# Group two's down projection in seven products, with weight sums made in group one's FFN

## The chip, the cores and the metric

The kernel runs on one core of one Trainium2 chip. Its engines work side by side from queues of their own: TensorE (PE: matmuls, PEld: the loading of their weights), VectorE (DVE), ScalarE (ACT), GpSimd (POOL) and SyncE (SP), which issues most DMA transfers. The metric is the device time of one execution in microseconds (us), lower is better; the number of a kernel is the median of its runs.

## The reference

One layer of an encoder with two attention mixers, run for 1024 prompt rows and 32 sample rows with the same weights. The FFN at its end is what matters here (D_MODEL 1024, D_FF 4096, all float32):

```python
h = x + jnp.einsum('bld,de->ble', m, w_out)
u = jnp.einsum('bld,df->blf', rmsnorm(h, g_ffn), w_up)
return h + jnp.einsum('blf,fd->bld', jnp.square(jax.nn.relu(u)), w_down)
```

## The kernel before

**Numbers.** TensorE works on pairs: each float32 operand is split into a high part h (a copy in the type float32r, made on ScalarE) and a low part l = x - h (made on POOL or VectorE). A product of 128 x 128 weights with a slice of activations is three matmuls (`three`): wh·xh, wh·xl, wl·xh. A weight *block* is 128 partitions x 512: four such 128 x 128 tiles. Blocks are loaded by SyncE to a raw tile (`wst`, bufs=3), then split to `wh`, `wl` (a ring of WB = 5 pairs).

**Groups.** The 1056 rows are run in two groups: group one has 512 rows (one slice of 512 columns), group two 544 (two slices c = 0, 1 of 272). Group one's FFN runs (`ffn_group`) while part of group two's attention (`late`) is fed in beside it, a piece each few blocks (`beside`). Then come group two's branch and output projections and its FFN.

**Group one's FFN.** Eight rounds q. Ups: a row of u is 8 x 3 matmuls of 512 columns into one of two PSUM banks (`pj`), relu and the rest on ScalarE, POOL (`ru`) and VectorE (`xl`). Downs: `go_down(e, q)` adds 512 rows of D_FF (four tiles, 12 matmuls) and VectorE adds the bank to the output tile y.

**Group two's FFN.** Its ups (`go_up_quad`) are done in the Strassen-Winograd form: a 2 x 2 quad of weight blocks times the two halves of the activations and the two slices is seven products of 12 matmuls instead of eight. That needs four sums of weight blocks (`quad_units`): they are made by loading a block by SyncE and adding others to it with accumulating transfers from POOL's queue (tile `raw`, bufs=10). The activations' sums (`g.sums`) are made once. Downs are plain: 8 x 8 x 2 of 12 matmuls into banks `pd`. One up quad and four downs alternate.

**Order.** Nothing is issued by hand. `Plan` records every instruction with a rank (FAST for what frees a bank, PREP for weights, MAIN, FILL for matmuls) and an estimated cost, and then issues for each engine the ready one of the best rank; it counts POOL and those VectorE instructions that have all inputs on chip (`locks`) as excluding each other. The order is fixed when the kernel is built; each engine keeps to it.

Of the kernel before, what the change touches and what calls it, by code (L numbers as in the profile page):

```python
# [19 lines left out]
D = 1024  # L20
# [21 lines left out]
WB = 5  # L42
SPLIT = 6
AHEAD = 0
KEEP = (6, 7)
# [373 lines left out]
class Layer:  # L419
# [9 lines left out]

    def split(self, h, l, x):  # L430

        self.nc.scalar.copy(h, x)
        self.nc.gpsimd.tensor_sub(l, x, h.bitcast(F32))
# [40 lines left out]
    def column_block(self, units, rhs, done, chunks, kn=KB, tag="pj"):  # L474

        nc = self.nc
        for c, cs in enumerate(chunks):
            n = cs.stop - cs.start
            ps = self.bank(tag)
            with nc.rank(FILL):  # L480
                for k in range(kn):
# [3 lines left out]
                    self.three(ps[:, :n], wh[:, ks], wl[:, ks], xh, xl, k == 0, k == kn - 1)  # L485
            with nc.rank(FAST):
                done(c, cs, ps[:, :n])
# [9 lines left out]
    def run(self):  # L497
# [34 lines left out]
        self.dh = dt([KB, 128, T], "dh")  # L532

# [104 lines left out]
        self.ffn_group(g2)  # L638
# [745 lines left out]
    def quad_units(self, f):  # L1384

        nc, a, w = self.nc, self.a, self.quads
        with nc.rank(PREP):
            src = lambda i, j: a["w_up"][f + i, j]
# [11 lines left out]
            def part(z, pool, tag, bufs, eng):  # L1400
                h = nc.tile(pool, [128, 512], F32R, tag + "h", bufs=bufs)
                l = nc.tile(pool, [128, 512], F32R, tag + "l", bufs=bufs)
                nc.scalar.copy(h, z)
                eng.tensor_sub(l, z, h.bitcast(F32))
                return h, l

            V, G = nc.vector, nc.gpsimd
            z = load((1, 0), (1, 1))
            z3 = load((0, 0), (1, 0))
            a11, a22, a12 = load((0, 0)), load((1, 1)), load((0, 1))  # L1410
            s1 = part(z, w, "s", 4, V)
            load((0, 0), out=z)
            s2 = part(z, w, "s", 4, V)
            load((0, 1), out=z)
            s3 = part(z3, w, "s", 4, V)
            s4 = part(z, w, "s", 4, G)
            p11 = part(a11, self.wpool, "w", WB, G)
            p12 = part(a12, self.wpool, "w", WB, G)
            p22 = part(a22, self.wpool, "w", WB, G)
        return p11, p12, p22, s1, s2, s3, s4  # L1420

# [10 lines left out]
    def square(self, g, ps, uh, ul, sign=1.0):  # L1432

        nc = self.nc
        r = g.tmp("ru", "pb", 3)
        nc.scalar.activation(r, ps, AF.Relu, scale=sign)
        if not g.i:
            nc.gpsimd.tensor_mul(r, r, r)
            nc.scalar.copy(uh, r)
            nc.vector.tensor_sub(ul, r, uh.bitcast(F32))  # L1440
            return
        nc.vector.scalar_tensor_tensor(ps, ps, sign, r, op0=ALU.mult, op1=ALU.mult)
        nc.scalar.copy(uh, ps)
        nc.vector.tensor_sub(ul, ps, uh.bitcast(F32))

    def ffn_group(self, g, late=iter(())):
        nc, a, i = self.nc, self.a, g.i
        n = g.n
        rb2 = g.acc

        def scales():

            for c in range(len(g.chunks)):
                ps = self.bank("pj")
                nc.tensor.matmul(ps[:, :n], self.ones, g.acc[c], start=True, stop=True)
                with nc.rank(FAST):
                    v = g.tmp("rv", "pb", 3)
                    nc.vector.tensor_scalar(v, ps[:, :n], 1.0 / D, EPS, op0=ALU.mult, op1=ALU.add)
                    nc.vector.reciprocal(rb2[c], v)

        nq, us = DFF // 512, {}

        def go_up(f):
            units = [self.unit(a["w_up"][f, j]) for j in range(2)]
            us[f] = uh, ul = g.mh[:, f % 8], g.ml[:, f % 8]
            self.column_block(units, lambda k, cs: (g.h[:, k, cs], g.l[:, k, cs]),
                              lambda c, cs, ps: self.square(g, ps, uh[:, cs], ul[:, cs]), g.chunks)

        def go_up_quad(f):

            a11, a12, a22, s1, s2, s3, s4 = self.quad_units(f)
            for i in range(2):
                us[f + i] = g.mh[:, (f + i) % 8], g.ml[:, (f + i) % 8]
            ta, tb, tc, td = ([(th[:, k], tl[:, k]) for k in range(4)] for th, tl in g.sums)
            x = lambda j, c: [(g.h[:, 4 * j + k, c * n:c * n + n], g.l[:, 4 * j + k, c * n:c * n + n]) for k in range(4)]

            def product(w, xs, ps=None):
                first = ps is None
                if first:
                    ps = self.bank("pj")[:, :n]  # L1480
                with nc.rank(FILL):
                    for k in range(4):
                        ks = slice(k * 128, k * 128 + 128)
                        self.three(ps, w[0][:, ks], w[1][:, ks], *xs[k], first and k == 0, k == 3, skip_group_check=True)
                return ps

            def keep(ps):
                t = nc.tile(self.op, [128, g.w], F32, "part", tag="o32", bufs=4)[:, :n]
                with nc.rank(FAST):
                    nc.scalar.copy(t, ps)  # L1490
                return t

            def done(i, c, out, ps, more=None):
                cs = slice(c * n, c * n + n)
                uh, ul = us[f + i]
                with nc.rank(FAST):
                    if more is not None:
                        nc.vector.tensor_add(out, ps, more)
                    self.square(g, out, uh[:, cs], ul[:, cs], -1.0 if i else 1.0)

            px = product(a11, x(0, 0))
            p1 = keep(px)
            pz = product(s1, ta)
            p5 = keep(pz)
            product(s2, tb, px)
            u2 = keep(px)
            product(s4, x(1, 1), pz)
            done(0, 1, pz, pz, u2)
            py = product(a12, x(1, 0))
            done(0, 0, py, py, p1)  # L1510
            product(s3, tc, px)
            done(1, 1, self.bank("pj")[:, :n], px, p5)
            product(a22, td, px)
            done(1, 0, px, px)

        def go_down(e, q):
            units = [self.unit(a["w_down"][e, q])]

            def done(c, cs, ps):
                y = g.y[:, e, cs]  # L1520
                if q == 0:
                    nc.scalar.copy(y, ps)
                    return
                if q < nq - 1:
                    nc.vector.tensor_add(y, ps, y)
                    return
                if e < KB // 2:
                    nc.vector.tensor_add(ps, ps, y)
                    y = hx_of(e, cs)
                nc.vector.tensor_mul(ps, ps, rb2[c])  # L1530
                nc.vector.tensor_add(g.y[:, e, cs], ps, y)
                nc.sync.dma_start(self.o["yT"][:, e, slice(g.lo + cs.start, g.lo + cs.stop)], g.y[:, e, cs])

            if q == nq - 1 and e >= KB // 2:
                for c, cs in enumerate(g.chunks):
                    y = g.y[:, e, cs]
                    nc.gpsimd.tensor_mul(y, y, rb2[c])
                    nc.gpsimd.tensor_add(y, y, hx_of(e, cs))
            self.column_block(units, lambda k, cs: (us[4 * q + k][0][:, cs], us[4 * q + k][1][:, cs]), done, g.chunks,
                              kn=4, tag="pd" if g.i else "pj")  # L1540

        def hx_of(e, cs):

            return g.h.bitcast(F32)[:, e, cs]

        def reload():

            with nc.rank(PREP):
                nc.sync.dma_start(g.h.bitcast(F32), self.dh[:, :, g.lo:g.lo + g.w].rearrange("e p t -> p e t"))
# [14 lines left out]
        if g.i:  # L1564
            go_up_quad(0)
            self.squares(g)
            go_up_quad(2)
            for q in range(nq):
                if q == 2:
# [106 lines left out]
```

## Time and profile before

| | us |
|---|---|
| median of three runs | 1766.61 (1764.76 to 1770.34) |
| the profiled execution | 1765.07 |
| its span, first to last instruction | 1763.3 |
| TensorE busy | 1739.2 (99%) |
| POOL / VectorE / ScalarE busy | 1051.8 / 1047.3 / 977.7 |

The granted TensorE clock is 1.00 throughout. Group one's FFN lies from about 860 to 1290 us, the late attention beside it until about 1115; group two's branch and output from 1290 to 1392, and its FFN from there to the end. Windows and groups of instructions are in us from the span's start; tiles have their names from the code, and nearly all instructions have the line of the one helper that issues them. Durations of matmuls overlap (they are pipelined), so their rate is read from counts.

### The profile page before, as it was taken

What the parts mean: (1) busy time and instruction counts of PE and PEld (TensorE: products, weight loads), DVE (VectorE), ACT (ScalarE), POOL (GpSimd) and SP (SyncE); (2) the same over time, 40 slices, a digit from 0 to 9 for tenths busy, and PEclk for the clock granted to TensorE, in tenths of its full rate; (3) what the DMA queues carried; (4) which work ended last, traced back from release to release, by engine and by line L of the source; (5) the groups of instructions that cost most, each with busy time, mean ns of one, the idle gap of its engine ahead of it and who ended that gap; (6) DMA issues with size and microseconds to landing.
All of it is one profiled execution on the core that took longest, in us unless ns stands there. A gap on an engine that the chain in (4) does not pass through costs nothing.

```text
span 1763.3 us, 32590 instructions
## 1 busy us (share of the span) xinstructions
PE 1739.2 (99%) x11394; PEld 1598.1 (91%) x11394; DVE 1047.3 (59%) x2284; ACT 977.7 (55%) x2145; POOL 1051.8 (60%) x902
## 2 busy tenths in 40 slices
PE   8999999999999999999999999999999999999999
PEld 7999999999899888888888888888899999999998
DVE  7555578999665645789646555222347853544445
ACT  7444598983255776677666455533336654444441
POOL 3623232435366675899965455675759876666655
PEclk9999999999999999999999999999999999999999
DMA  7244451545566668555444443433487576666624
GB/s 256 74 132 119 114 175 64 143 140 152 170 177 169 173 182 229 180 171 173 121 130 119 130 145 99 147 108 97 144 262 205 152 178 149 155 151 154 156 67 138
DMA packets 169908, 264.53 MB, mean 150 GB/s; under 512 B 28944, under 2 KB 58224, under 8 KB 169744
## 3 DMA queue, kind: packets, MB, share of 16 engines
q1 hardware_dynamic: 160096, 245.33, 47.4%
q0 software_dynamic: 9216, 16.78, 5.9%
q8 instruction: 90, 1.47, 0.3%
q14 instruction: 74, 0.61, 0.1%
q10 hardware_dynamic: 432, 0.34, 0.1%
HBM read 207.87 MB, written 54.40 MB: 149 GB/s over the span
## 4 chain that ended last, share of the span: by engine, by line
PE 87%; DMA 5%; DVE 2%; POOL 2%; issue 1%; ACT 1%; SPq 0%; POOLq 0%; ACTq 0%; DVEq 0%
PE pj L410 54%; PE s L410 13%; PE pd L410 11%; PE t L410 5%; PE o L410 4%; DMA raw<-w_up 1%; DMA sg<-dg 1%; POOL wl L410 1%; DMA k<-dk 1%; POOL pb L410 1%; SPq L410 0%; DMA o<-do 0%; DMA xt<-x 0%; DVE pen L410 0%; DMA q<-dq 0%
## 5 line engine op out<-in xcount | busy, mean ns | idle before, releaser
L410 POOL TENSOR_TENSOR wl<-wst,wh 128x512 fp32r<-128x512 f32 x350 | 493.4, 1419 | 359.7 <-ACT wh L410 334.8
L410 PE MATMUL pj<-xh,wh 128*128 128x512 f32 (+1 forms) x1600 | 557.5, 349 | 0.4 <-DVE vt L410 0.3
L410 PE MATMUL pj<-xh,wl 128*128 128x512 f32 (+1 forms) x1600 | 557.0, 349 | 0.0
L410 PE MATMUL pj<-xl,wh 128*128 128x512 f32 (+1 forms) x1600 | 556.7, 348 | 0.1
L410 ACT CAST wh<-wst 128x512 fp32r<-128x512 f32 x350 | 216.7, 621 | 324.3 <-PE pj L410 158.8
L410 PEld LDWEIGHTS pj<-xh,wh 128*128 128x128 f32 x1600 | 300.8, 188 | 33.6 <-ACT xh L410 0.7
L410 PEld LDWEIGHTS pj<-xh,wl 128*128 128x128 f32 x1600 | 300.8, 188 | 33.2
L410 PEld LDWEIGHTS pj<-xl,wh 128*128 128x128 f32 x1600 | 301.1, 188 | 32.0 <-DVE xl L410 0.3
L410 PE MATMUL pd<-xh,wh 128*128 128x272 f32 x512 | 148.3, 290 | 0.6 <-ACT y L410 0.3
L410 PE MATMUL pd<-xl,wh 128*128 128x272 f32 x512 | 147.5, 288 | 0.0
L410 PE MATMUL pd<-xh,wl 128*128 128x272 f32 x512 | 147.2, 288 | 0.0
L410 DVE TENSOR_TENSOR tt<-t,tt 128x512 fp32r<-128x512 f32 (+2 forms) x168 | 100.5, 622 | 62.1 <-ACT tt L410 60.6
L410 ACT ACTIVATE junk<-score,cand 128x384 bf16<-128x384 f32 (+1 forms) x124 | 116.0, 936 | 9.8 <-DVE cand L410 7.7
L410 DVE TENSOR_TENSOR_SCAN rem<-rem 128x896 f32<-128x896 f32 (+6 forms) x66 | 114.7, 1762 | 10.3 <-ACT rem L410 9.9
L410 POOL TENSOR_TENSOR p<-p,rem 128x895 f32<-128x895 f32 (+6 forms) x66 | 100.5, 1537 | 24.7 <-DVE rem L410 24.6
L410 ACT CAST tt<-t 128x512 fp32r<-128x512 f32 (+2 forms) x168 | 85.2, 540 | 45.7 <-PE t L410 38.7
L410 PE MATMUL s<-wl,xh 128*128 128x256 f32 (+1 forms) x360 | 101.8, 285 | 0.2 <-POOL wl L410 0.2
L410 PE MATMUL s<-wh,xh 128*128 128x256 f32 (+1 forms) x360 | 100.3, 286 | 0.9 <-DVE small L410 0.7
L410 PE MATMUL s<-wh,xl 128*128 128x256 f32 (+1 forms) x360 | 100.8, 283 | 0.0
L410 PEld LDWEIGHTS o<-tt,v 128*128 128x128 f32 x640 | 93.3, 188 | 8.3
L410 PE MATMUL s<-k,q 128*128 128x384 f32 (+5 forms) x384 | 96.1, 357 | 4.5 <-DMA q<-dq 1.6
L410 PE MATMUL o<-tt,v 128*128 128x256 f32 (+1 forms) x640 | 98.8, 276 | 0.0
(259 smaller groups left out, 3845.4 us busy)
## 6 DMA issues: line engine op xcount, KB each, us to landing
wst<-w_down SPq DMA_DIRECT2D x128, 256.0 KB, 2.7
raw<-w_up SPq DMA_DIRECT2D x80, 256.0 KB, 3.0
q<-dq SPq DMA_DIRECT2D x64, 256.0 KB, 5.4
wst<-w_up SPq DMA_DIRECT2D x64, 256.0 KB, 2.6
raw<-w_up POOLq DMA_DIRECT2D x64, 256.0 KB, 4.5
k<-dk SPq DMA_DIRECT2D x48, 256.0 KB, 4.2
v<-dv SPq DMA_DIRECT2D x48, 256.0 KB, 3.9
wst<-w_g SPq DMA_DIRECT2D x42, 256.0 KB, 3.4
```

Source lines behind the costliest of these rows:

```text
L410: fn(*args, **kw)
```

## The change

- **Group two's downs** are done in seven products too (`ffn_quads`, with `up` and `down`). They work on sums of u's parts: after each up quad the seven sets U11, T1, T2, U22, T3, U21, T4 are made from the products and split (`parts`), in place of four. A down block i is seven products over 512 rows each, so 1024 rows of D_FF and 2 x 2 output tiles at a time; its seven results are gathered in y. The rounds become four: four up quads, then four down blocks.
- **The weight sums** of both matrices are made in group one's FFN (`sums`): VectorE adds the four raw blocks in place, four additions of 128 x 512 for each quad, 128 in all, and SyncE stores the four results to DRAM, 128 stores of 256 KB. Group two loads them like weights, 224 plain loads by SyncE; the 64 accumulating transfers of POOL's queue are gone.
- **Group one's FFN** takes its blocks in quads (`row`), the raw blocks from a ring of eight tiles (three `wst`, three `sg`, two halves of `rb`), and its downs 1024 rows deep (24 matmuls for a bank); VectorE adds to y in three rounds in place of seven. KEEP, which held two downs back, is gone.
- Group two's raw blocks turn through nine tiles (the same eight and one `raw`), its split pairs through seven (five `wh`/`wl` and two `sh`/`sl`), and the banks `pj` and `pd` through one ring of eight.

```diff
-    def quad_units(self, f):
-            def load(*blocks, out=None):
-                st = out
-                if out is None:
-                    st = nc.tile(w, [128, 512], F32, "raw", bufs=10)
-                    nc.sync.dma_start(st, src(*blocks[0]))
-                    blocks = blocks[1:]
-                for b in blocks:
-                    nc.gpsimd.dma_start(st, src(*b), accum_op=ALU.add)
-                return st
...
+    def late_scale(self, g, e, c, cs, ps, sign=1.0, out=None):
+        (nc.vector.tensor_add if sign > 0 else nc.vector.tensor_sub)(out, y, ps)
+        nc.vector.tensor_mul(out, out, g.acc[c])
+        nc.vector.tensor_add(y, out, g.h.bitcast(F32)[:, e, cs])
+        nc.sync.dma_start(self.o["yT"][:, e, slice(g.lo + cs.start, g.lo + cs.stop)], y)
...
+    def ffn_quads(self, g):
...
+        def weights(name, t, engs):
+            w11, w12, _, w22 = (a[name][i, t] for i in range(4))
+            s1, s2, s3, s4 = self.sums[name, t]
+            for z, eng in zip((w11, s1, s2, s4, s3, w12, w22), engs):
+                with nc.rank(PREP):
+                    wt = pair(load(z), eng)
+                yield wt
...
+        def up(q, j):
+            wt = weights("w_up", 4 * q + j, (G, V, G, G, V, G, G))
...
+            px = product(next(wt), x[0])
+            keep(p1, px)
+            pz = product(next(wt), x[1])
+            keep(p5, pz)
+            product(next(wt), x[2], px)
+            keep(u2, px)
+            product(next(wt), x[3], pz)
+                add(pz, pz, u2)
+                square(u12, pz, 1.0)
+            product(next(wt), x[4], px)
+            pw = turn("bank", banks)
+                add(pw, px, p5)
+                square(pw, pw, -1.0)
+                parts(U22[j], pw, V)
+                sub(pz, pw, u12)
+                parts(T3[j], pz, V)
+            py = product(next(wt), x[5])
+                add(py, py, p1)
+                square(py, py, 1.0)
+                parts(U11[j], py, V)
+                sub(t1, py, u12)
+                parts(T1[j], t1, G)
+                V.scalar_tensor_tensor(t2, t1, -1.0, pw, op0=ALU.mult, op1=ALU.subtract)
+                parts(T2[j], t2, G)
+            product(next(wt), x[6], px)
+                square(px, px, -1.0)
+                parts(U21[j], px, V)
+                V.scalar_tensor_tensor(px, t2, -1.0, px, op0=ALU.mult, op1=ALU.subtract)
+                parts(T4[j], px, V)
...
+        def down(q, i):
+            wt = weights("w_down", 4 * q + i, (V, G, V, G, V, G, V))
...
+            px = product(next(wt), u[0])
+            gather(0, 0, px, 1.0, 0)
+            pz = product(next(wt), u[1])
+            gather(1, 1, pz, -1.0, 0)
...
+            product(next(wt), u[6], px)
+            gather(1, 0, px, -1.0, 2)
+
+        for q in range(4):
+            for j in range(4):
+                up(q, j)
+                if q + j == 0:
+                    self.squares(g)
...
+            for i in range(4):
+                down(q, i)
...
+        def sums(name, t, w11, w12, w21, w22):
+            add = nc.vector.tensor_add
+            add(w22, w21, w22)
+            add(w21, w11, w21)
+            add(w11, w11, w22)
+            add(w12, w12, w11)
+            for out, z in zip(self.sums[name, t], (w22, w11, w21, w12)):
+                nc.sync.dma_start(out, z)
...
+        for q in range(4):
+            for go, name, step in ((lambda j, i, w: go_up(4 * i + j, w), "w_up", 1),
+                                   (lambda j, i, w: go_down(2 * j + i, q, w), "w_down", 0)):
...
+                for j in range(4):
+                    raw = []
+                    for i in range(2):
+                        st, units = row(name, 4 * q + j, i)
+                        raw += st
+                        go(j, i, units)
+                        beside(2)
...
+                    sums(name, 4 * q + j, *raw)
```

The two weight matrices are laid out in quads on the host (the same numbers in another order).

How the order moves, at three places. **VectorE, group one's downs.** Before, it had there only the additions to y and, for the ups, the low part of u (`xl<-ru,xh`):

```order
L410 TENSOR_TENSOR y_6537<-pj,y_6537 128x512
L410 TENSOR_TENSOR xl_95<-ru,xh_94 128x512
L410 TENSOR_TENSOR y_6537<-pj,y_6537 128x512 x5
L410 TENSOR_TENSOR xl_95<-ru,xh_94 128x512 x2
L410 TENSOR_TENSOR y_6537<-pj,y_6537 128x512
```

Now, in a down stretch without attention (raw, wst and rb are the tiles of the raw blocks):

```order
L409 TENSOR_TENSOR y_6665<-pj,y_6665 128x512 x2
L409 TENSOR_TENSOR raw<-wst,raw 128x512
L409 TENSOR_TENSOR wst<-wst 128x512
L409 TENSOR_TENSOR wst<-wst,raw 128x512
L409 TENSOR_TENSOR wst<-wst 128x512
L409 TENSOR_TENSOR y_6665<-pj,y_6665 128x512 x2
L409 TENSOR_TENSOR rb<-rb 128x512
L409 TENSOR_TENSOR rb<-raw,rb 128x512
L409 TENSOR_TENSOR raw<-raw,rb 128x512
L409 TENSOR_TENSOR raw<-raw 128x512
```

Four sums stand between each two additions to y, all with both inputs on chip.

**SyncE, group one's FFN.** Before, weights were loaded one after another, beside the attention's q, k, v and its stores do:

```order
L410 DMA do<-o 64x512
L410 DMA wst<-w_up 128x512 x3
L410 DMA wst<-w_down 128x512 x2
L410 DMA do<-o 64x512
L410 DMA wst<-w_down 128x512 x2
L410 DMA k<-dk 128x512 x2
```

Now (dw_up and dw_down are the sums in DRAM):

```order
L409 DMA dw_up_0_138<-rb 128x512
L409 DMA dw_up_2_140<-rb 128x512
L409 DMA dw_up_1_139<-raw 128x512
L409 DMA dw_up_3_141<-raw 128x512
L409 DMA rb<-w_up 128x512 x2
L409 DMA raw<-w_up 128x512 x2
L409 DMA dw_up_0_142<-raw 128x512
L409 DMA dw_up_2_144<-wst 128x512
```

The loads to a ring's tiles stand behind the stores of the sums that lay in them.

**VectorE, group two's FFN.** Before, a quad's steps lay among the downs' additions (`y<-pd,y`):

```order
L410 TENSOR_TENSOR y_14410<-pd,y_14410 128x272 x6
L410 TENSOR_TENSOR sl<-raw,sh 128x512
L410 TENSOR_TENSOR pj<-pj,part 128x272 x2
L410 SCALAR_TENSOR_TENSOR pj<-pj,ru 128x272
L410 TENSOR_TENSOR pj<-pj,part 128x272
L410 SCALAR_TENSOR_TENSOR pj<-pj,ru 128x272
L410 TENSOR_TENSOR xl_95<-pj,xh_94 128x272
```

Now, in a stretch of ups (ut and ut2 hold u's parts that are kept, ul and xl the low parts of the sets):

```order
L409 TENSOR_TENSOR pj<-pj,part 128x272
L409 TENSOR_TENSOR ut<-pj,ut 128x272
L409 TENSOR_TENSOR wl<-wst,wh 128x512
L409 SCALAR_TENSOR_TENSOR pj<-pj,ru 128x272
L409 TENSOR_TENSOR pj<-pj,ut 128x272
L409 SCALAR_TENSOR_TENSOR ut_16511<-ut,pj 128x272
L409 TENSOR_TENSOR wl<-rb,wh 128x512
L409 TENSOR_TENSOR xl_223<-pj,xh_222 128x272
L409 TENSOR_TENSOR ul<-pj,uh 128x272
L409 SCALAR_TENSOR_TENSOR pj<-pj,ru 128x272
```

No downs lie between a quad's steps; the next quad's steps and weights do. TensorE has 192 matmuls less in the whole list.

More of the change, by code (lines that the diff above doesn't have):

```diff
@@ L428, in bank, with turn @@
         return self.nc.tile(self.pp[tag], [128, 512], F32, tag, tag="pj" if tag == "pd" else tag, bufs=n)
+    def turn(self, what, ways):
+        n = self.turns.get(what, 0)
+        self.turns[what] = n + 1
+        return ways[n % len(ways)]()
     def split(self, h, l, x):
@@ L480, in column_block @@
             with nc.rank(FILL):
-                for k in range(kn):
+                for i, k in enumerate(order or range(kn)):
                     wh, wl = units[k // 4]
@@ L532, in run @@
         self.dh = dt([KB, 128, T], "dh")
+        self.sums = {(w, t): [dt([128, 512], f"d{w}{t}_{i}") for i in range(4)] for w in ("w_up", "w_down") for t in range(16)}
+        self.turns = {}
         self.wpool = nc.open("w")
@@ L1430, in squares, with scales @@
                 self.nc.gpsimd.tensor_add(g.ss, g.ss, y)
-    def square(self, g, ps, uh, ul, sign=1.0):
+    def scales(self, g):
         nc = self.nc
[L1435 to L1488, printed above, removed]
@@ new lines, in scales, with reload @@
+        for c in range(len(g.chunks)):
+            ps = self.bank("pj")
+            nc.tensor.matmul(ps[:, :g.n], self.ones, g.acc[c], start=True, stop=True)
+            with nc.rank(FAST):
+                v = g.tmp("rv", "pb", 3)
+                nc.vector.tensor_scalar(v, ps[:, :g.n], 1.0 / D, EPS, op0=ALU.mult, op1=ALU.add)
+                nc.vector.reciprocal(g.acc[c], v)
+    def reload(self, g, n=1):
+        with self.nc.rank(PREP):
+            for es in (slice(0, 2), slice(2, KB)) if n > 1 else (slice(0, KB),):
+                self.nc.sync.dma_start(
+                    g.h.bitcast(F32)[:, es], self.dh[es, :, g.lo:g.lo + g.w].rearrange("e p t -> p e t"))
@@ new lines, in late_scale, with load, pair, product @@
+    def late_scale(self, g, e, c, cs, ps, sign=1.0, out=None):
+        nc = self.nc
+        y = g.y[:, e, cs]
+        out = ps if out is None else out
+        (nc.vector.tensor_add if sign > 0 else nc.vector.tensor_sub)(out, y, ps)
+        nc.vector.tensor_mul(out, out, g.acc[c])
+        nc.vector.tensor_add(y, out, g.h.bitcast(F32)[:, e, cs])
+        nc.sync.dma_start(self.o["yT"][:, e, slice(g.lo + cs.start, g.lo + cs.stop)], y)
+    def ffn_quads(self, g):
+        nc, a, w, n = self.nc, self.a, self.quads, g.n
+        V, G, add, sub = nc.vector, nc.gpsimd, nc.vector.tensor_add, nc.vector.tensor_sub
+        turn = self.turn
+        raws = [lambda: nc.tile(self.wpool, [128, 512], F32, "wst", bufs=3)] * 3
+        raws += [lambda: nc.tile(w, [128, 512], F32, "raw", bufs=1)]
+        raws += [lambda: self.rb[:, 0:512], lambda: self.rb[:, 512:1024]]
+        raws += [lambda: nc.tile(self.op, [128, g.w], F32, "raw", tag="sg", bufs=3)[:, :512]] * 3
+        pairs = [lambda: [nc.tile(self.wpool, [128, 512], F32R, z, bufs=WB) for z in ("wh", "wl")]] * WB
+        pairs += [lambda: [nc.tile(w, [128, 512], F32R, z, bufs=2) for z in ("sh", "sl")]] * 2
+        banks = [lambda: self.bank("pj")[:, :n]] * 6 + [lambda: self.bank("pd")[:, :n]] * 2
+        def load(src):
+            st = turn("raw", raws)
+            nc.sync.dma_start(st, src)
+            return st
+        def pair(st, eng):
+            h, l = turn("pair", pairs)
+            nc.scalar.copy(h, st)
+            eng.tensor_sub(l, st, h.bitcast(F32))
+            return h, l
+        def weights(name, t, engs):
[5 more added lines that the diff above has]
+                yield wt
+        def product(wt, xs, ps=None):
+            first = ps is None
+            if first:
+                ps = turn("bank", banks)
+            with nc.rank(FILL):
+                for k in range(4):
+                    ks = slice(k * 128, k * 128 + 128)
+                    self.three(ps, wt[0][:, ks], wt[1][:, ks], *xs[k], first and k == 0, k == 3, skip_group_check=True)
+            return ps
+        ta, tb, tc, td = ([(th[:, k], tl[:, k]) for k in range(4)] for th, tl in g.sums)
+        x = lambda j, c: [(g.h[:, 4 * j + k, c * n:c * n + n], g.l[:, 4 * j + k, c * n:c * n + n]) for k in range(4)]
+        x = [x(0, 0), ta, tb, x(1, 1), tc, x(1, 0), td]
+        old = [z.rearrange("p k t -> p (k t)").rearrange("p (i k t) -> p i k t", i=4, k=4) for z in (g.mh, g.ml)]
+        new = [nc.tile(w, [128, 3, 4, n], F32R, z) for z in ("uh", "ul")]
+        sets = [[z[:, i] for z in old] for i in range(4)] + [[z[:, i] for z in new] for i in range(3)]
+        u = [[(h[:, k], l[:, k]) for k in range(4)] for h, l in sets]
+        U11, T1, T2, U22, T3, U21, T4 = u
+        def parts(place, z, eng):
+            nc.scalar.copy(place[0], z)
+            eng.tensor_sub(place[1], z, place[0].bitcast(F32))
+        half = lambda name: nc.tile(self.op, [128, g.w], F32, name, tag="o32", bufs=4)
+        def up(q, j):
+            wt = weights("w_up", 4 * q + j, (G, V, G, G, V, G, G))
+            two, three_ = half("part"), half("ut")
+            u12, t1 = three_[:, :n], three_[:, n:]
+            t2 = half("ut2")
+            t2, u2 = t2[:, :n], t2[:, n:]
+            p1, p5 = two[:, :n], two[:, n:]
+            def keep(t, ps):
@@ L1502, in go_up_quad, with square @@
[L1502 to L1517, printed above, removed]
+            def square(out, ps, sign):
+                r = g.tmp("ru", "pb", 3)
+                nc.scalar.activation(r, ps, AF.Relu, scale=sign)
+                V.scalar_tensor_tensor(out, ps, sign, r, op0=ALU.mult, op1=ALU.mult)
```

175 lines of the change are left out of this document (88 added, 87 removed).

## The prediction

> **What bounds the kernel now.** I read the page's totals first, then its chain, then the windows, because a total says nothing of a stage.
>
> ```profile
> span 1763.3 us, 32590 instructions
> PE 1739.2 (99%) x11394; PEld 1598.1 (91%) x11394; DVE 1047.3 (59%) x2284; ACT 977.7 (55%) x2145; POOL 1051.8 (60%) x902
> PE 87%; DMA 5%; DVE 2%; POOL 2%; issue 1%; ACT 1%; SPq 0%; POOLq 0%; ACTq 0%; DVEq 0%
> ```
>
> TensorE is busy 99% of the span and 87% of the chain that ends last. A busy TensorE need not be one at its rate, so the windows (length; PE, PEld, DVE, ACT and POOL busy with counts; granted clock; DMA share; GB/s) must give the rate in the two stages that the change touches.
>
> ```profile
> 1200.00:1250.00 50.00, 50.00 (x222) 41.41 (x221) 13.14 (x15) 15.59 (x27) 29.12 (x24) 1.00 0.35 100
> 1300.00:1350.00 50.00, 48.30 (x379) 47.44 (x377) 25.60 (x46) 23.93 (x46) 37.93 (x38) 1.00 0.82 238
> 1400.00:1450.00 50.00, 48.11 (x373) 46.88 (x373) 29.98 (x48) 28.88 (x71) 39.34 (x34) 1.00 0.77 171
> 1440.00:1720.00 280.00, 280.00 (x2229) 279.69 (x2228) 119.65 (x263) 127.56 (x282) 166.92 (x145) 1.00 0.61 139
> ```
>
> Group one's FFN, once the late attention is out of it, runs one 512-column matmul each 50/222 = 225 ns; group two's runs one 272-column matmul each 280/2229 = 125.6 ns with no gap for 280 us. There a matmul less is worth 125.6 ns, whatever its recorded duration. The chain says the same: ups (pj) and downs (pd) alternate at 126 and 125 ns a matmul.
>
> ```profile
> 1553.38 8.92 PE pj L410 x71
> 1568.46 7.51 PE pd L410 x60
> ```
>
> The other engines have room in group two (DVE 43%, ACT 46%, POOL 60%). Only its beginning has gaps: 1.7 us idle in 1300 to 1350 and 1.9 us in 1400 to 1450.
>
> **The removal.** Group two's downs are
>
> ```profile
> L410 PE MATMUL pd<-xh,wh 128*128 128x272 f32 x512 | 148.3, 290 | 0.6 <-ACT y L410 0.3
> raw<-w_up POOLq DMA_DIRECT2D x64, 256.0 KB, 4.5
> 1309.02 11.20 DMA sg<-dg
> 1406.20 3.96 DMA raw<-w_up
> 1418.86 4.39 DMA raw<-w_up
> 1428.97 4.56 DMA raw<-w_up
> ```
>
> three such groups, 1536 matmuls. Seven products for 16 blocks of twelve matmuls are 16 x 7 x 12 = 1344. So 192 go: 192 x 125.6 ns = **24.1 us**. The ups keep their 1344, group one its 3 x 896.
>
> The 64 accumulating transfers on POOL's queue go too. At the start of the FFN they are links in the chain: load, add, split, and only then a matmul (the rows at 1406, 1419 and 1429). Their first ones also stand beside the gate loads of the branch stage, one of which takes 11.2 us to land. The sums are now ready in DRAM, so one plain load replaces such a chain. I bound this gain by 0 and by the 3.6 us of the two gaps, and take **2.0 us**, since half of them should have other causes.
>
> **The additions in group one.** 128 additions of 128x512 on VectorE, both inputs on chip, and 128 stores. The nearest rows, in the windows 1120 to 1290 (the last stretch without attention):
>
> ```profile
> L410 POOL TENSOR_TENSOR wl<-wst,wh 128x512 fp32r<-128x512 f32 x62 | 80.9, 1311 | 52.7 <-ACT wh L410 52.5
> L410 POOL TENSOR_TENSOR ru<-ru 128x512 f32<-128x512 f32 x15 | 15.6, 1043 | 0.0
> L410 DVE TENSOR_TENSOR xl<-ru,xh 128x512 fp32r<-128x512 f32 x15 | 20.5, 1367 | 63.7 <-ACT xh L410 63.7
> L410 DVE TENSOR_TENSOR y<-pj,y 128x512 f32<-128x512 f32 x28 | 19.4, 691 | 50.0 <-PE pj L410 49.8
> ```
>
> An addition from PSUM takes 691 ns. The one from two on-chip tiles (xl) takes 1367 there, though this timeline has it at 0.68 where POOL had been idle and at 1.37 where a POOL subtraction had begun 0.47 us before:
>
> ```profile
> 940.01 0.68 DVE L410 TENSOR_TENSOR xl<-ru,xh 128x512 fp32r<-128x512 f32 x1
> 941.38 1.13 POOL L410 TENSOR_SCALAR p<-p,nb 128x1024 f32<-128x1024 f32 x1 [1.82 <-PE pj L410]
> 1175.94 1.30 POOL L410 TENSOR_TENSOR wl<-wst,wh 128x512 fp32r<-128x512 f32 x1 [0.43 <-ACT wh L410]
> 1176.41 1.37 DVE L410 TENSOR_TENSOR xl<-ru,xh 128x512 fp32r<-128x512 f32 x1 [8.46 <-ACT xh L410]
> ```
>
> It ends 0.54 us after POOL's: it waited for POOL, so I count the two as taking turns. Per quad of four weight blocks TensorE needs 48 x 225 = 10.8 us. In an up quad the turns are 4 wl x 1.31 + 2 ru x 1.04 on POOL, and 2 xl x 0.68 + 4 sums x 0.69 on VectorE: 7.3 + 4.1 = 11.4 us, 0.6 over. In a down quad 5.2 + 2.8 = 8.0 us, 2.8 under. The split weights run five pairs ahead, 5 x 12 x 225 ns = 13.5 us of TensorE's work, more than four up quads fall behind (2.4 us). So it is covered by that lead; without it 16 x 0.6 = 10 us. Against the sums stand 32 evacuating additions that the 1024-deep downs save (0.69 each, 22 us of VectorE, from PSUM). The other place without cover is the start of that FFN, where POOL has no idle time:
>
> ```profile
> 840.00:850.00 10.00, 10.00 (x56) 8.66 (x56) 8.47 (x9) 6.62 (x14) 10.00 (x6) 1.00 0.53 168
> ```
>
> The first two quads' sums, 8 x 0.69 = 5.5 us, fall about there. Both together cost 0 to 15 us; I take **1.5**, because TensorE loses next to nothing at 840 to 850 though POOL is full. The stores, 128 x 256 KB over some 430 us, are 78 GB/s on top of the 100 at 1200 to 1250, less than the 238 GB/s of 1300 to 1350.
>
> The Trainium skill, SBUF — State Buffer, section "Who interferes with whom", states that a VectorE instruction with two SBUF inputs contends with a GpSimd one that reads SBUF, and that the later one blocks fully. That agrees with the 1.37 against 0.68 us above, and it speaks against this change: by it every sum is taken from POOL's time or POOL's from it.
>
> **The new order in group two.** Ups and downs no longer alternate: four up quads (84 matmuls, 10.5 us each), then four down blocks. What an up quad asks of each engine, from these rows:
>
> ```profile
> L410 DVE TENSOR_TENSOR sl<-raw,sh 128x512 fp32r<-128x512 f32 x36 | 25.6, 732 | 48.1 <-ACT sh L410 41.0 <-PE pj L410 7.0
> L410 DVE SCALAR_TENSOR_TENSOR pj<-pj,ru 128x272 f32<-128x272 f32 x49 | 21.5, 440 | 3.6 <-ACT ru L410 3.6
> L410 POOL TENSOR_TENSOR wl<-raw,wh 128x512 fp32r<-128x512 f32 x36 | 47.3, 1326 | 13.6 <-ACT wh L410 13.5
> L410 POOL TENSOR_TENSOR xl<-raw,xh 128x272 fp32r<-128x272 f32 x12 | 11.1, 946 | 0.0
> L410 ACT CAST wh<-raw 128x512 fp32r<-128x512 f32 x36 | 22.4, 622 | 25.0 <-issue 13.6 <-PE pj L410 5.5 <-POOL sl L410 2.5
> L410 ACT CAST xh<-pj 128x272 fp32r<-128x272 f32 x49 | 18.7, 384 | 0.5 <-DVE pj L410 0.4
> 1423.33 1.14 ACT L410 CAST sh<-raw 128x512 fp32r<-128x512 f32 x2 [1.68 <-DMA raw<-w_up]
> ```
>
> ScalarE: 7 casts of weights x 622 + 14 narrow ones (3 keeps, 4 relus, 7 casts) x 384 = 9.7 us of 10.5 by durations; two casts in 1.14 us show that they overlap by a tenth, so rather 8.8. VectorE: 2 x 0.73 + 16 x 0.44 = 8.5 us. POOL: 5 x 1.33 + 2 x 0.95 = 8.5 us, and with VectorE's two taking turns 10.0 us. Every one is under 10.5, none by much. In a down block the same sums are 4.4 (ScalarE), 4 x 0.73 + 7 x 0.44 = 6.0 (VectorE) and 3 x 1.33 = 4.0 us (POOL). A stretch of ups draws on seven split pairs, a quad's worth, so throughput is covered.
>
> What is less covered is the wait that opens inside a quad. The fifth product adds into a bank, VectorE reads it (add(pw, px, p5)), and the seventh adds into the same bank; between them stand the sixth product or the next quad's first, 12 x 125.6 ns = 1.5 us. That read stands on VectorE behind a weight subtraction, and these can be long where POOL is full:
>
> ```profile
> L410 DVE TENSOR_TENSOR sl<-raw,sh x48: 674/688/4162, 1308.9 to 1699.5; 128x512 fp32r<-128x512 f32 x48
> 1406.81 2.83 POOL L410 TENSOR_TENSOR wl<-raw,wh 128x512 fp32r<-128x512 f32 x2
> 1406.90 3.30 DVE L410 TENSOR_TENSOR sl<-raw,sh 128x512 fp32r<-128x512 f32 x1
> ```
>
> A median of 0.69 us costs nothing. One of 3.3 us delays the read past its 1.5 us by some 2 us. In the order a weight subtraction is among the three instructions ahead of that read in five of the 16 quads. I bound the loss by 0 and by 1 us in every quad, 16 us, and take **2.0 us**, 0.4 in each of the five: nearer to the median than to the long ones, since POOL no longer issues transfers there.
>
> **Sum**, against the profiled execution: span 1763.3 - 24.1 - 2.0 + 1.5 + 2.0 = 1740.7, and 1.8 us lie around it (1765.07 - 1763.3), 1742.5. The median of the runs, 1766.6, is 1.5 us above the profiled execution; I say **1743 us**. The end keeps its form: a last product, two VectorE steps and a store.
>
> **The rivals.** *The up stretches are bound by VectorE behind POOL.* For it: 10.0 of 10.5 us in turns, and 4.16 us as the longest subtraction. Against it: 280 us without a gap with the same seven products. Half the full price to all of it, 8 to 16 us: 1749 to 1757, say 1753.
>
> *VectorE and POOL taking turns bind group one.* By that port rule taken as a mechanism of this kernel, nothing is hidden: 10 us in the up quads and 5 at the start instead of 1.5, 1743 + 13.5 = 1756. For it: 11.4 against 10.8 us. Against: the down quads, and the lead. That is the rule of the skill's page named above; its time comes from the rows.
>
> *Slower: SyncE's queue in group one.* There each load of a raw block stands behind the stores of sums, which wait for VectorE, which waits for POOL; late, it holds up the next loads, the attention's among them. With eight raw buffers a quad's round must close within two quads, 21.7 us.
>
> ```profile
> wst<-w_down SPq DMA_DIRECT2D x128, 256.0 KB, 2.7
> dh<-y SPq DMA_DIRECT2D x8, 256.0 KB, 2.9
> ```
>
> Load 2.7, cast 0.6, four subtractions 5.2, sums 4 x 1.37 = 5.5 if each waits for POOL, store 2.9: 16.9 us. Above 21.7 every us costs one in two quads, 16 in all. The gain is eaten at 23.2; at 23.8 the kernel takes 1743 + 34 = 1777 us. For it: in 780 to 870 VectorE and POOL are nearly full. Against it: 4.8 us of slack, and quads that last longer while attention is mixed in.
>
> *More than I count:* both beginnings cleared and no new wait, 1765.1 - 24.1 - 3.6 = 1737.
>
> **Chances.** The forecast with its terms at their near ends (1738 to 1748) 0.58, the first rival 0.16, the second 0.09, slower 0.06, more 0.05; 0.06 is left for mixtures of the rivals that just cancel the gain. A measurement of this kernel tells 0.3%, 5.3 us, from no change: below 1761.3 is faster, so 0.88 faster, 0.06 the same, 0.06 slower. The range reaches from the favourable end to the second rival: 1735 to 1758.
>
> **What would show it.** 11202 matmuls, TensorE at 125.6 ns through all of group two, the time from the first up to the last down near 340 us, no accumulating transfers, sums at 0.7 to 1.4 us, and group one's FFN as long as before. Wrong would be: TensorE waiting for VectorE (pj) inside up stretches, for POOL's wl in group one, or SyncE's queue waiting for VectorE with wst landing late.

## The result, and the profile after

The changed kernel takes 1743.5 us (median of four runs, 1742.1 to 1745.5), the kernel before beside it 1765.7 (1763.4 to 1770.3): a ratio of 0.9872, with an interval of 0.9849 to 0.9895. Eight runs of the changed kernel, four of them taken later beside other experiments, have the same median. The profiled execution's span is 1741.1 us. The page's totals and the head of its chain:

```profile
span 1741.1 us, 32989 instructions
PE 1715.7 (99%) x11202; PEld 1574.6 (90%) x11202; DVE 1228.1 (71%) x2496; ACT 1018.6 (59%) x2241; POOL 1054.3 (61%) x862
PE 87%; DVE 5%; DMA 3%; issue 2%; POOL 2%; ACT 1%; SPq 0%; ACTq 0%; POOLq 0%; DVEq 0%
```

192 matmuls are gone, VectorE has 181 us more work, and TensorE is 99% busy as before. Three markers cut the span into stages: the first matmul of group two's branch (pj<-gh, by tile, before and then after), and the first copy of a product in group two's FFN (part<-pj):

```profile
L410 PE MATMUL pj<-gh,wh x34: 284/288/297, 1292.2 to 1304.6; 128*128 128x272 f32 x34
L410 ACT COPY part<-pj x6: 377/388/395, 1394.4 to 1407.7; 128x272 f32<-128x272 f32 x6
```

```profile
L409 PE MATMUL pj<-gh,wh x20: 284/288/297, 1297.5 to 1304.6; 128*128 128x272 f32 x20
L409 ACT COPY part<-pj x4: 381/390/394, 1395.8 to 1408.6; 128x272 f32<-128x272 f32 x4
```

| stage | before | after | difference |
|---|---|---|---|
| up to group two's branch | 1292.2 | 1297.5 | +5.3 |
| branch and output of group two | 102.2 | 98.3 | -3.9 |
| group two's FFN, to the span's end | 368.9 | 345.3 | -23.6 |
| span | 1763.3 | 1741.1 | -22.2 |

The same number of matmuls (7742) stands ahead of the first marker in both. So the forecast of 1743 was met by a sum of which two terms were badly sized, and these cancelled. The windows after, in the columns of the prediction's:

```profile
1150.00:1160.00 10.00, 8.82 (x39) 6.96 (x38) 6.96 (x6) 2.92 (x5) 10.00 (x7) 1.00 0.58 191
1160.00:1170.00 10.00, 8.86 (x39) 6.86 (x38) 7.35 (x5) 3.59 (x7) 10.00 (x8) 1.00 0.54 180
1200.00:1250.00 50.00, 50.00 (x222) 41.42 (x221) 32.88 (x29) 18.10 (x32) 39.26 (x29) 1.00 0.57 194
1300.00:1350.00 50.00, 50.00 (x400) 50.00 (x399) 24.83 (x46) 23.39 (x45) 36.19 (x34) 1.00 0.67 200
1350.00:1400.00 50.00, 50.00 (x400) 50.00 (x399) 35.49 (x48) 32.88 (x70) 38.71 (x34) 1.00 0.64 184
1400.00:1450.00 50.00, 49.12 (x388) 48.56 (x387) 39.66 (x81) 36.92 (x92) 41.88 (x34) 1.00 0.60 176
1420.00:1430.00 10.00, 9.23 (x73) 8.94 (x71) 7.44 (x15) 6.74 (x18) 10.00 (x9) 1.00 0.48 131
1440.00:1720.00 280.00, 279.42 (x2201) 277.26 (x2200) 185.86 (x382) 167.41 (x373) 160.65 (x137) 1.00 0.62 184
1520.00:1530.00 10.00, 9.72 (x73) 9.07 (x72) 8.66 (x23) 6.95 (x19) 4.34 (x6) 1.00 0.55 162
```

What to read here are the counts, not the busy time. A group two window of 50 us holds 400 matmuls when nothing is late. After, 1300 to 1400 is full; before, it had 379 and 395, and 1400 to 1450 had 373. Group one lost seven matmuls in 1150 to 1160 and six in 1160 to 1170 (39 where 46 and 45 stood before). There TensorE waits for POOL, as its waits in 1120 to 1298 and then the chain say:

```profile
PE pj L409 <- POOL wl L409: 2.3, 2, 1.2
```

```profile
1149.82 1.75 POOL wl L409
1151.57 1.45 POOL ru L409
1153.02 1.68 POOL wl L409
1154.70 0.04 issue
1154.74 5.34 PE pj L409 x22
```

```profile
1148.66 1.75 DVE L409 TENSOR_TENSOR wst<-wst 128x512 f32<-128x512 f32 x1
1150.45 1.68 DVE L409 TENSOR_TENSOR wst<-wst,raw 128x512 f32<-128x512 f32 x1
1152.16 1.41 DVE L409 TENSOR_TENSOR wst<-wst 128x512 f32<-128x512 f32 x1
1153.70 1.54 DVE L409 TENSOR_TENSOR xl<-ru,xh 128x512 fp32r<-128x512 f32 x1
```

VectorE's timeline (the last fence) and POOL's chain interlock: each instruction takes 1.4 to 1.75 us while the other engine has one under way. By groups, 1120 to 1290, POOL's low parts last longer and a sum takes well over the 0.69 us of an addition from PSUM:

```profile
L409 POOL TENSOR_TENSOR wl<-raw,wh 128x512 fp32r<-128x512 f32 x24 | 35.5, 1488 | 16.8 <-ACT wh L409 16.8
L409 POOL TENSOR_TENSOR wl<-wst,wh 128x512 fp32r<-128x512 f32 x22 | 34.8, 1600 | 8.4 <-ACT wh L409 8.4
L409 POOL TENSOR_TENSOR ru<-ru 128x512 f32<-128x512 f32 x16 | 19.4, 1211 | 6.4 <-ACT ru L409 6.3
L409 DVE TENSOR_TENSOR wst<-wst 128x512 f32<-128x512 f32 x16 | 18.4, 1147 | 0.5
```

Something else stands ahead of the two late low parts. `gl`, the low part of group two's attention output, takes POOL twice in a row before each (one line of POOL's timeline for each pair):

```profile
1146.24 3.62 POOL L409 TENSOR_TENSOR gl<-o,gh 128x544 fp32r<-128x544 f32 x2
1158.60 3.62 POOL L409 TENSOR_TENSOR gl<-o,gh 128x544 fp32r<-128x544 f32 x2
```

From the one pair to the next 12.4 us pass, in which POOL does two gl, four wl and two ru without a pause. TensorE needs 10.8 us for such a quad.

### The profile page after: what moved, and what is told of

Its sections match the earlier page's. It is cut to its first block, busy times and chain, and to the rows that moved or that the text cites. A ratio compares the mean times of both kernels' runs of the same rounds, so it can differ in the third digit from the quotient of the medians.

```text
span 1741.1 us, 32989 instructions
## 1 busy us (share of the span) xinstructions
PE 1715.7 (99%) x11202; PEld 1574.6 (90%) x11202; DVE 1228.1 (71%) x2496; ACT 1018.6 (59%) x2241; POOL 1054.3 (61%) x862
## 4 chain that ended last, share of the span: by engine, by line
PE 87%; DVE 5%; DMA 3%; issue 2%; POOL 2%; ACT 1%; SPq 0%; ACTq 0%; POOLq 0%; DVEq 0%
PE pj L409 63%; PE s L409 13%; PE t L409 5%; PE o L409 4%; PE pd L409 2%; POOL wl L409 1%; DVE xl L409 1%; DMA q<-dq 1%; DVE rem L409 0%; DMA o<-do 0%; DVE pen L409 0%; DMA x<-xT 0%; SPq L409 0%; DVE wst L409 0%; DMA k<-dk 0%
## 5 line engine op out<-in xcount | busy, mean ns | idle before, releaser
L409 PE MATMUL pj<-xh,wl 128*128 128x512 f32 (+1 forms) x1872 | 636.4, 340 | 2.3 <-POOL wl L409 2.3
L409 PE MATMUL pj<-xh,wh 128*128 128x512 f32 (+1 forms) x1872 | 636.0, 340 | 0.6 <-DVE vt L409 0.3
L409 PE MATMUL pj<-xl,wh 128*128 128x512 f32 (+1 forms) x1872 | 634.8, 340 | 0.0
L409 POOL TENSOR_TENSOR wl<-wst,wh 128x512 fp32r<-128x512 f32 x237 | 351.0, 1488 | 227.3 <-ACT wh L409 210.5
L409 PEld LDWEIGHTS pj<-xh,wl 128*128 128x128 f32 x1872 | 352.0, 188 | 37.0 <-POOL wl L409 3.7
L409 PEld LDWEIGHTS pj<-xh,wh 128*128 128x128 f32 x1872 | 352.1, 188 | 35.1 <-ACT xh L409 0.9
L409 ACT CAST wh<-wst 128x512 fp32r<-128x512 f32 x260 | 160.2, 622 | 152.9 <-PE pj L409 104.1
L409 POOL TENSOR_TENSOR wl<-raw,wh 128x512 fp32r<-128x512 f32 x78 | 113.5, 1460 | 64.3 <-ACT wh L409 45.6
L409 ACT CAST wh<-raw 128x512 fp32r<-128x512 f32 x118 | 73.4, 625 | 85.6 <-PE pj L409 45.2
L409 POOL TENSOR_TENSOR p<-p,rem 128x895 f32<-128x895 f32 (+6 forms) x66 | 101.8, 1557 | 22.2 <-DVE rem L409 22.1
L409 PE MATMUL pj<-gh,wh 128*128 128x272 f32 x320 | 92.4, 289 | 0.0
```

What stands on the lines that cost most here:

```text
L409: fn(*args, **kw)
```

## The experiments

Two theories stood at the beginning. *Turns:* the additions cost the 5 us in group one, because VectorE and POOL exclude each other while both read tiles on chip. *Queue or order:* it is the stores behind which SyncE's loads stand, or the new order of group one's FFN itself.

### The additions, the stores, both

Left out were the additions and the stores (group two then loads plain blocks in place of the sums), the additions alone, and the stores alone (here too group two loads plain blocks).

```diff
 def sums(name, t, w11, w12, w21, w22):
-    add(w22, w21, w22)      # e2: these four lines go, the stores stay
-    add(w21, w11, w21)      # e3: these stay, the stores go
-    add(w11, w11, w22)      # e1: both go
-    add(w12, w12, w11)
-    for out, z in zip(self.sums[name, t], (w22, w11, w21, w12)):
-        nc.sync.dma_start(out, z)
```

> Leaves out the 128 additions and the 128 stores of group one; group two loads plain weight blocks where it loaded sums, as many as before. The changed kernel took 1743.5 us, and its group one FFN, from the first relu to the first matmul of group two's branch, grew from 434.3 to 440.9 us. Theory A (additions and POOL take turns): the 6.6 us come back, group one near 434, kernel near 1737. Theory B (the stores and loads in SyncE's queue, or the traffic): the same here, 1737. Theory C (the new order of group one's FFN, quads and deep downs, whatever the sums cost): stays at 440 and 1743.

> Keeps the 128 stores, of the raw blocks, and leaves out the 128 additions. Theory A: group one near 434 and 1737 to 1738 us, as without both; POOL's wl back at about 1.31 us. Theory B: stays near 441 and 1743. Theory C: 1743.

> Keeps the 128 additions and leaves out the 128 stores (group two loads plain blocks in their place). Theory A: stays near 440 and 1743 us, POOL's wl near 1.49 us. Theory B: group one near 434, 1737 us. Theory C: 1743.

Measured: 1738.8 us without both (ratio to the kernel before 0.9838, 0.9819 to 0.9856), 1737.7 without the additions (0.9836, 0.9816 to 0.9856), 1743.3 without the stores (0.986, 0.9839 to 0.9881). By these medians the additions cost what the changed kernel has over the runs without them, 5 to 6 us; the 128 stores, the traffic and the new order cost nothing that shows there. In the run with the stores alone the two windows are full again:

```profile
1150.00:1160.00 10.00, 10.00 (x46) 8.29 (x45) 2.12 (x2) 4.30 (x8) 10.00 (x9) 1.00 0.64 198
1160.00:1170.00 10.00, 10.00 (x46) 8.29 (x45) 2.50 (x3) 3.40 (x6) 7.02 (x6) 1.00 0.65 191
```

But they are nearly full without the stores too, where every addition is there and POOL is as full:

```profile
1150.00:1160.00 10.00, 10.00 (x45) 8.29 (x45) 7.19 (x5) 4.90 (x10) 10.00 (x8) 1.00 0.36 112
1160.00:1170.00 10.00, 10.00 (x45) 8.26 (x44) 8.62 (x6) 4.00 (x7) 10.00 (x7) 1.00 0.34 106
```

In that run's order the gl steps do not come in pairs here (they begin at 1144.2, 1147.4, 1157.0 and 1168.1). So the stall at 1150 and 1165 takes more than the additions; that it is the pairs of gl is read from the order and had no run of its own.

How much of the 5 to 6 us lies where the additions are? Matmuls can be counted off in the trace in order of their start. The 5200th begins before any addition (the first begins at 847 us, the first reduction of the next section at 829 us):

| profile | 5200th matmul | from there to group two's branch |
|---|---|---|
| the kernel before | 799.6 | 492.6 |
| the changed kernel, twice, and with an eighth product (below) | 799.9, 801.3, 803.0 | 497.6, 496.5, 496.5 |
| additions alone | 802.6 | 494.9 |
| additions of the down weights alone (below) | 802.4 | 493.8 |
| without both, stores alone, reductions (below) | 798.6, 799.7, 797.6 | 493.2, 492.5, 492.8 |

Behind the count the changed kernel has 3.3 to 5.1 us more than the runs without additions, the run with the additions alone 1.7 to 2.4 us. By the profiles, then, the stores or the order that comes with them have a part in it, which the medians do not show. The rest of the difference between these profiles lies ahead of the first addition and is not the additions' work; the last section comes back to it.

### VectorE's time, or the turns

That still leaves two readings: VectorE's time and place in its queue, or the turns. In place of each addition stands a reduction of the same block to 128x1, one block read on chip instead of two; the stores stay and write the blocks as they are, so the sums are left out.

```diff
-            add(w22, w21, w22)
-            add(w21, w11, w21)
-            add(w11, w11, w22)
-            add(w12, w12, w11)
+            for z in (w22, w21, w11, w12):
+                nc.vector.reduce_sum(self.scrap, z, axis=AX.X)
```

> The changed kernel with each of the 128 additions replaced by an instruction of VectorE on the same 128x512 block that reads one block on chip and writes 128x1 (a reduction to its row sums; the sums are thus left out, the stores stay and write the blocks as they are). If what costs is that VectorE and GpSimd take turns while an addition reads two blocks on chip, the reductions last 0.5 to 0.7 us, GpSimd's wl goes back to 1.3 us, and the time is that of the run with the stores alone, 1737.5 to 1739. If what costs is VectorE's time and its place in the queue beside attention (0.6 us an instruction, 128 times), 1741 to 1743.5. Half of both: 1740.

Measured: 1737.0 us (1735.7 to 1739.1; 0.9837, 0.9822 to 0.9851), the time without any additions. The groups in 1120 to 1290:

```profile
L409 POOL TENSOR_TENSOR wl<-wst,wh 128x512 fp32r<-128x512 f32 x24 | 30.8, 1291 | 14.2 <-ACT wh L409 14.1
L409 POOL TENSOR_TENSOR wl<-raw,wh 128x512 fp32r<-128x512 f32 x22 | 28.4, 1295 | 23.0 <-ACT wh L409 22.9
L409 POOL TENSOR_TENSOR ru<-ru 128x512 f32<-128x512 f32 x16 | 16.7, 1042 | 0.8 <-ACT ru L409 0.4 <-DMA raw<-w_up 0.2
L409 DVE TENSOR_REDUCE scrap<-wst 128x1 f32<-128x512 f32 x21 | 14.4, 684 | 0.6
L409 DVE TENSOR_REDUCE scrap<-raw 128x1 f32<-128x512 f32 x21 | 14.3, 683 | 15.7 <-DMA raw<-w_up 8.2 <-DMA raw<-w_down 7.2
```

An instruction of 0.68 us in the place of each sum costs nothing; wl is back at 1.29 us from 1.49 to 1.60. So it isn't the 128 instructions on VectorE that cost, but that each of them reads two tiles on chip while POOL does. The Trainium skill, SBUF — State Buffer, section "Who interferes with whom", states just this distinction (a VectorE instruction with two SBUF inputs contends with a GpSimd one that reads SBUF; one with at most one SBUF input, outside VectorE's 2-port modes, does not). This pair of runs agrees with both halves.

A reduction also writes no block, which would be another reading. The kernel before speaks against it: its additions to y (y<-pj,y) read one tile on chip and write a block, and all 28 of them in 1120 to 1290 have a POOL instruction beside them and last 0.68 to 0.69 us; the wl that have only such an addition beside them keep 1.29 us (median of 17). What this pair of runs can't separate is the order, which `Plan` makes anew for each of them.

### Which additions

The additions of the up weights are left out; their stores stay and write the blocks as they are.

```diff
+            if name == "w_down":
                 add(w22, w21, w22)
                 add(w21, w11, w21)
                 add(w11, w11, w22)
                 add(w12, w12, w11)
```

> The changed kernel with the additions of the up weights left out (their stores stay and write the blocks as they are, so group two's ups multiply wrong sums); the 64 additions of the down weights stay. The prediction charged the loss to the up quads (11.4 us of turns against 10.8) and to the first two quads, and gave the down quads 2.8 us to spare: then this gets back all of the 5 to 6 us that the additions cost, 1738. If the loss is spread evenly over all additions: 1740.5 to 1741. If it sits in the down quads beside attention: 1743.

Measured: 1740.3 us (1737.1 to 1741.8; 0.9847, 0.9829 to 0.9864). Half of the additions left out gives back 3.2 us by the medians. By the table above this run is 2.7 to 3.8 us below the changed kernel behind the count and 0.6 to 1.3 above the runs without any additions. So most of the price hangs on the up additions. Whether the down additions cost anything is not shown: the intervals of this run and of the one without any additions overlap.

### Taking work from POOL

Two trials of a cure for the turns, with all of the work done: group one's square (32 multiplications on POOL) goes from POOL to VectorE, from PSUM (first), or to ScalarE, on chip (second).

```diff
-                nc.gpsimd.tensor_mul(r, r, r)
-                nc.scalar.copy(uh[:, cs], r)
-                nc.vector.tensor_sub(ul[:, cs], r, uh.bitcast(F32)[:, cs])
+                nc.vector.scalar_tensor_tensor(ps, ps, 1.0, r, op0=ALU.mult, op1=ALU.mult)
+                nc.scalar.copy(uh[:, cs], ps)
+                nc.vector.tensor_sub(ul[:, cs], ps, uh.bitcast(F32)[:, cs])
```

```diff
-                nc.gpsimd.tensor_mul(r, r, r)
+                nc.scalar.activation(r, r, AF.Square)
```

> All the work is done; group one's square moves from POOL (32 multiplications of 1.04 us on chip) to VectorE, which multiplies the PSUM bank by its relu, and the low part is subtracted from PSUM too, so neither has two on-chip inputs. Theory A: an up quad's turns fall from 11.4 to 5.2 + 2.8 = 8.0 us, under TensorE's 10.8; group one loses the two waits for wl in its late up stretch and comes to 435 to 437, kernel 1738 to 1740. Theory B and C: group one stays at 440; if VectorE, which gets 32 x 0.69 us more, holds the two banks, it grows: 1743 to 1748.

> The changed kernel in full, with one edit: group one's square of the relu goes from GpSimd to ScalarE (in place, on chip), so that GpSimd keeps 64 multiplications of 1.0 to 1.2 us fewer and VectorE gets none in their place. Theory (GpSimd and VectorE take turns, and the loss sits where GpSimd's wl is late and where VectorE is nearly full beside attention): this relieves GpSimd without the load on VectorE that undid the earlier trial of squaring there; the two waits for wl at 1150 and 1165 go, 3 to 4 us faster than the changed kernel, 1739 to 1741. Rival (any instruction that leaves GpSimd is paid for elsewhere in the attention stretch): 1743.

> The changed kernel once more, unedited, on the same chip as the two runs beside it, so that the differences of 2 to 3 us can be told from the scatter of single executions (1742.1 to 1745.5 in four runs). Expected 1743.5 by either theory.

> The kernel with group one's square on ScalarE once more, beside the changed kernel: five runs reached from 1739.0 to 1746.2, too wide to tell 1743.3 from 1741. Turns theory: its profile has 0.3 us of waits for wl where the changed kernel has 2.3, so 1.5 to 3 us less than the changed kernel beside it. Rival (paid for elsewhere): within 1 us of it.

Measured: 1743.0 us with the square on VectorE (0.9856, 0.9836 to 0.9877). With it on ScalarE 1743.3 and, again, 1741.6 (0.9857, 0.9841 to 0.9874), beside 1743.5 for the changed kernel (0.9871, 0.9855 to 0.9887). All nine runs of the ScalarE form have a mean of 1742.2, all eight of the changed kernel 1743.5: 1.3 us less, with an interval, from drawing anew among the runs, of 3.1 less to 0.6 more. Neither is shown to beat the changed kernel. Yet the waits for wl went: none in the first (1120 to 1298), 0.3 us in the second (2.3 in the changed kernel). In the first others came, beside the attention, in 860 to 1120:

```profile
PE pj L409 <- DVE xl L409: 1.3, 2, 1.0
```

From the 5200th matmul to group two's branch the first takes 496.7 us and the second 494.5 and 496.4, where the runs without additions take 492.5 to 493.2. So the wait that the profile names in the changed kernel isn't the whole price of the additions; it is where that price shows in one order of the instructions. Where the ScalarE form loses the rest was not settled.

### The price of the removal

An eighth product comes back into each down block: the last product's twelve matmuls once more, into a bank that nobody reads.

```diff
-            product(next(wt), u[6], px)
+            w7 = next(wt)
+            product(w7, u[6], px)
             gather(1, 0, px, -1.0, 2)
+            product(w7, u[6])
```

> Group two's down blocks get an eighth product: the last product's twelve matmuls are issued once more, into a bank of their own that nobody reads, 16 x 12 = 192 matmuls of 272 columns more; the output does not change, nothing else is added. The prediction's price of the removal (192 x 125.6 ns) says this brings back 24.1 us: 1767 to 1768 us, the kernel before within 2 us. Rival: the down blocks of the new order have idle time in them (waits of TensorE that the added matmuls would fill), and then it costs clearly less, 15 to 20 us.

Measured: 1767.9 us (1.0 us above the kernel before, ratio 1.0004, 0.9994 to 1.0015), 24.3 us more than the changed kernel (23.3 by the two ratios to the kernel before), with 11394 matmuls again. The 192 matmuls cost 23 to 24 us; idle time in the down blocks swallowed next to nothing.

### The accumulating transfers

In the kernel before, the 64 accumulating transfers are left out, so each sum is only its first block.

```diff
-                for b in blocks:
-                    nc.gpsimd.dma_start(st, src(*b), accum_op=ALU.add)
```

> The kernel before, with the 64 accumulating transfers on GpSimd's queue left out and nothing in their place (each weight sum is then only its first block, so the part left out is the summation). Group one has no additions either, the products stay those of the kernel before. If those transfers are what made the branch stage and the first quad of group two longer, as the windows 1290 to 1410 say, this is 3 to 7 us faster than the kernel before. If the prediction's 2.0 us was right and the rest of the gain came from the new order, 2 us. If only the order of the loads matters, 0.

Measured: 1760.2 us, 6.7 less than the kernel before (0.9964, 0.995 to 0.9978). The windows:

```profile
1300.00:1350.00 50.00, 50.00 (x400) 50.00 (x399) 29.96 (x52) 27.03 (x53) 37.01 (x34) 1.00 0.72 233
1350.00:1400.00 50.00, 50.00 (x399) 50.00 (x398) 37.14 (x46) 33.01 (x70) 41.34 (x35) 1.00 0.55 161
1400.00:1450.00 50.00, 50.00 (x400) 50.00 (x399) 26.69 (x51) 31.93 (x79) 31.68 (x25) 1.00 0.41 122
```

400, 399 and 400 matmuls in place of 379, 395 and 373: 52 x 0.125 = 6.5 us. Those transfers cost the kernel before more than three times what the prediction gave them. Only 21 of the 64 are issued up to 1450. From 1440 to 1720, where most of the others lie, leaving them out gives nothing (2230 matmuls for 2229). In the branch stage a gate load (sg<-dg) takes up to 12.1 us to land in the kernel before, up to 6.3 without the transfers and up to 4.4 in the changed kernel. Which part of a transfer does it (POOL's 0.9 us for issuing one, its bytes, or the first quad's wait for it) was not separated.

## Why the prediction was right

**The removal, -24.1:** right. The eighth product put back costs 23 to 24 us.

**The start of group two, -2.0, bounds 0 and 3.6:** the mechanism was right, the size wrong, and the true value lay outside the bounds. Leaving the transfers out gives 6.7 us. In the two profiles the branch stage is 3.9 us shorter, and 1400 to 1450 has 15 matmuls more (1.9 us), although it now holds the new loss below. The step that failed is "the 3.6 us of the two gaps": idle time was read where counts should have been. The prediction's own rows had 379 and 373 matmuls in 50 us, and at its own pitch of 125.6 ns 50 us hold 398; those 44 missing matmuls are 5.5 us, of which busy time shows 3.6; the ends of matmuls are modelled in the profile, so a short stall can hide in them. The weight loads (PEld) of the same two rows, busy 47.44 and 46.88 of 50 us where a full window has 50.00, would have shown 5.7.

**Group one, +1.5, bounds 0 and 15:** mis-sized; +5.3 in the profiles, 5.0 of it behind the 5200th matmul, and 5 to 6 us by the medians of the runs without the additions. The mechanism named there, turns, is what the reduction shows. What failed is the ledger by quads and its cover: "more than four up quads fall behind ... So it is covered by that lead". The ledger charged each engine with the durations of an undisturbed instruction, 0.69 for a sum and 1.31 for wl; in the turns the means of their groups are 1.10 to 1.31 and 1.35 to 1.60. And it left gl out, though the kernel before has eight of them between 1132 and 1160 (1.38 to 1.84 us each). With two gl the up quad at 1146 took POOL 12.4 us, not under TensorE's 10.8, and TensorE needed 3.3 us more for the 200 matmuls around the two waits than in the run without both. In the run without the stores, where no pair of gl stands ahead of these weights, the profile has about half the price. That the down quads' additions were free by this ledger is not contradicted.

**The new order in group two, +2.0:** near in size, wrong in place. In 1440 to 1720 there are 2201 matmuls where there were 2229: 28 x 0.125 = 3.5 us. No loss stands at the reads inside the up quads: 1530 to 1600 and 1620 to 1690 run at one matmul per 125 ns.

```profile
1530.00:1600.00 70.00, 70.00 (x559) 70.00 (x558) 42.58 (x87) 39.04 (x84) 40.01 (x33) 1.00 0.60 174
1620.00:1690.00 70.00, 70.00 (x559) 70.00 (x558) 43.45 (x89) 40.86 (x90) 42.69 (x37) 1.00 0.60 177
```

It stands where the ups pass into the downs (1420 and 1520 above: 73 matmuls where a full 10 us counts 82; the two later passes, in 1610 to 1620 and 1690 to 1700, have 77). At 1430 the last up quad waits for a weight pair whose sl is third in a row on POOL (the waits of TensorE put 0.9 us to it). At 1527 it is the first down block, and the chain comes from the last up quad's parts, which wait on VectorE behind a weight's sl:

```profile
1426.36 1.54 POOL wl L409
...
1428.05 0.77 POOL xl L409
1428.82 1.25 POOL sl L409
```

```profile
1524.66 0.69 DVE sl L409
1525.36 0.35 DVE xl L409
1525.71 0.36 DVE pj L409
1526.06 0.34 DVE ul L409
1526.40 0.36 DVE ut L409
...
1526.78 0.40 ACT xh L409
```

So the parts of u that a down block needs at once have no other product between them and their use there; the prediction looked only at the bank that the fifth and seventh product share. This is read from the trace; no run took it away.

**The rivals.** VectorE behind POOL binding the ups (1753) fell with the full stretches. Turns binding group one (1756) is the mechanism that acted, at less than half of its price. SyncE's queue (1777) fell: taking the stores away left the median where it was. "More than I count" (1737) is what the kernel takes without the additions.

**The sum.** -24.1 - 2.0 + 1.5 + 2.0 had its errors in opposite directions: the start gave 4 to 5 us more than counted, the additions took some 4 more and the new order 1.5. That the total was met within 1 us is luck beyond the first term.

## What to carry to other kernels

Read a TensorE-bound stage by matmuls per window against the count of a full window, and place a difference in its stage before giving it a cause: busy time hid a third of the stalls at the start of group two, and the missing counts come near to what leaving the transfers out gained. Before work is moved to VectorE beside a busy GpSimd, look at how many of its inputs lie on chip: with one, 128 instructions of 0.68 us were free here, and with two they cost some 4 to 6 us in a kernel whose VectorE was 29% idle. A wait that disappears after an edit isn't yet a gain: twice here the named wait went and the median hardly moved.

## What the runs showed that was not expected

Accumulating transfers on GpSimd's queue held up their neighbours far more than themselves: the first 21 of them made a stretch of 150 us 6.5 us longer, half of it in the branch and output stage, which doesn't use what they bring; the other 43 cost nothing that shows.

Executions differ by some 3 us and more long before any changed work. In 400 to 850 the runs without both (first row) and with the additions alone (second) have the same instructions in the same order up to 836 us, and

```profile
400.00:850.00 450.00, 444.24 (x2864) 402.13 (x2862) 315.11 (x545) 269.16 (x646) 318.55 (x241) 1.00 0.63 179
```

```profile
400.00:850.00 450.00, 442.10 (x2835) 399.60 (x2834) 312.70 (x543) 266.65 (x639) 314.33 (x238) 1.00 0.61 175
```

29 matmuls lie between them, some 4 us. Of TensorE's waits there, those for loads of q and k differ (2.5 and 4.8 us); they land at other times in each execution. The profiles of all three runs without additions are early ones here (798 to 800 us at the 5200th matmul, the changed kernel 800 to 803). Whether that is chance, and how far it enters their medians of four executions, stays open. So a difference of 3 us between two profiles must be placed in a stage before it is put down to an edit, and group one's stage can't be compared by its end alone.
